# A norm's gain and bias loaded in turned form, and a pinned product moved ahead of `pv`

## The chip, the core and the metric

The kernel runs on one core of a Trainium2 chip. The metric is the device time of one execution in microseconds. The profile names the engines PE (TensorE, the matrix products), DVE (VectorE), ACT (ScalarE), POOL (GpSimd) and SP (SyncE, which issues most of the DMAs).

## The reference, cut to what matters

One encoder layer in float32: a state-space mixer and a gated MLP mixer over chunks of 128 positions, merged by gates; then cross-attention to a memory; then a SwiGLU feed-forward. The sequence has 512 rows of 1024 channels. The change touches the gated mixer's layer norm and the start of the feed-forward:

```python
def sgu_branch(zu, zv, ln_g, ln_b, w_s, bias):
    zu = jax.nn.gelu(zu)
    zv = layer_norm(jax.nn.gelu(zv), ln_g, ln_b)
    zv = zv.reshape(bsz, seq // CHUNK, CHUNK, SGU_HEADS, SGU_HEAD_DIM)
    sv = jnp.einsum('hts,bnshd->bnthd', w_s, zv) + bias.T[None, None, :, :, None]
    return zu * sv.reshape(bsz, seq, SGU_WIDTH)

def swiglu(hn, w_gate, w_up, w_down):
    return (jax.nn.silu(hn @ w_gate) * (hn @ w_up)) @ w_down
```

The mixing is linear, so the kernel applies the norm's gain `g` and bias `b` after it: `sv` is `g` times the mixed, normalised rows plus `mix`, and `mix` is `b` times the row totals of `w_s` plus `bias`. `g` and `b` have 1024 values each, 8 heads of 128 channels.

## The kernel before

**Products.** Each float32 weight is split in a high part `whi` (ScalarE, L85) and a low part `wlo` (DVE, L86), and each product is made of three: high-high, high-low, low-high (`mm3`, L376). Weights come in 512 KB blocks in a fixed list, `plan`; a block's load is issued three blocks ahead of its use (on SP's queue), and its split two blocks ahead. Tiles in PSUM are `pf` (products by features), `pt` (by tokens) and, in the feed-forward, `px`, `pv`, `pq`: the 256-column parts of products that are computed with seven instead of eight half-size products (`product`, L1252, 24 instructions each).

**Order.** Each engine runs its instructions in the order in which they stand in its own queue. That order is made when the kernel is built, by a scheduler that follows a modelled timeline; `in_order` pins an instruction to its place among the others so pinned, and `later(n, f)` writes a piece of code n ticks of product work further on. The order may therefore change far from an edit.

**The state-space side.** From 60 to 134 us, between the large products of `w_in`, each of eight groups goes the same way (`s5_inputs`, L948): DVE makes an operand in `wsx` (L983 twice, L987), PE turns it in two pieces `pw` (L961), ScalarE copies them to `wt`, PE multiplies them in one piece `pz` (L968; the trace shows each of the eight products as two matmuls), and ScalarE (L973) and DVE (L974) copy its two halves to `zh`. `pw`, `pz` and other small pieces share the PSUM pool `aux`, which has three banks (L81): a piece can begin when the piece three before it has been read. Then follows a scan on DVE (L992).

**Mixing.** The row totals of `w_s` (L1186) go through DRAM and come back as a broadcast to all partitions, `rsb`, which lies in the tile `squares` (L1190). `g` and `b` are loaded as 16 rows `gbr`, turned by PE (`pgb`) and copied to `gbc`, 128 partitions by 16. Eight DVE instructions (L1176) then make `mix` from `rsb`, `gbc` and the loaded bias; `psv` and `sv` (L1211) use it.

**Start of the feed-forward.** `gate_part` multiplies the rest of `w_gate` with the halves T0 and T1 of the tokens; `unit_start` and `unit_second` make `px` and `pv` of the first unit. `idle_product` (L1265) is one matmul whose result nobody reads, pinned behind `pv`.

Of the kernel before, what the change touches and what calls it, by code (L numbers as in the profile page):

```python
# [9 lines left out]
F32 = mybir.dt.float32  # L10
# [7 lines left out]
P = 128  # L18
# [11 lines left out]
H = 8  # L30
# [22 lines left out]
def hybrid_layer_kernel(  # L53
# [8 lines left out]
    nc = tc.nc  # L62
    x, mem, out = x[0], mem[0], out[0]
# [7 lines left out]
    np_ = ctx.enter_context(tc.tile_pool(name="norm", bufs=2))  # L71
# [5 lines left out]
    def bank(name):  # L77
        return pm.tile([P, 512], F32, tag="mm", name=name)

    def aux(name, shape=(P, 512)):  # L80
        return pa.tile(list(shape), F32, tag="aux", name=name)  # L81
# [12 lines left out]
    in_order = tc.keep_in_program_order  # L94
# [256 lines left out]
    def next_w(*key):  # L351
        i = used_w[0]
        used_w[0] += 1
        assert len(plan[i][0]) == len(key) and plan[i][0][1:] == key[1:] and plan[i][0][0] is key[0]
        for j in range(i, min(i + FAR + 1, len(plan))):
            begin(j, i)
            if j - 1 >= len(tiles) and j - 1 <= i + SPLITS:
                split_w(j - 1)
        for j in range(len(tiles), min(i + SPLITS + 1, len(plan))):
            split_w(j)  # L360
        tile_, tiles[i] = tiles[i], None
        return tile_
# [45 lines left out]
    def feat_block(ps, x, act, nk, kpt, tsl, fresh=True):  # L408

        kb, hi, lo = x  # L410
        for j in range(2):
            cs = slice(j * P, (j + 1) * P)
            for k in range(kpt):
                kk = kb + k
                mm3(ps[j][:, tsl], (hi[:, k, cs], lo[:, k, cs]), (act[0][:, kk, tsl], act[1][:, kk, tsl]),
                    kk == 0 and fresh, kk == nk - 1, not fresh)
# [45 lines left out]
    def later(n, fn):  # L462

        side["later"].append((side["now"] + n, fn))
# [7 lines left out]
    def tick(us=5.2):  # L472

        side["now"] += us / 5.2
        run_due()
        side["credit"] = min(side["credit"] + us * side["rate"], us)
        while side["credit"] > 0.0 and side["gen"] is not None:
            try:
                used = next(side["gen"])
            except StopIteration:  # L480
                side["gen"] = None
                return
            if used is None:
                side["credit"] = 0.0
                return
            side["credit"] -= used
# [8 lines left out]
    ident = cp.tile([P, P], F32, name="ident")  # L495
# [67 lines left out]
    def slot(tag, shape, dt, name, place=NEAR):  # L563
        n = math.prod(shape[1:])
        t = sp.tile([P, KD * T + ROOM[tag]], dt, tag=tag, name=name)[:, place[tag]:place[tag] + n]
        return t.rearrange("p (a b c) -> p a b c", a=shape[1], b=shape[2]) if len(shape) == 4 else (
            t.rearrange("p (a b) -> p a b", a=shape[1]))

    def token_slot(name, place=NEAR):
        return tuple(slot(tag, (P, KD, T), F32R, name, place) for tag in "BC")  # L570
# [584 lines left out]
        nc.scalar.activation(z, z, AF.Identity, bias=nm, scale=r)  # L1155

    nc.sync.dma_start(wsr, sgu_w[0].rearrange("h t s -> t h s"))
    gbr = np_.tile([2 * H, P], F32, tag="gain", name="gbr", bufs=2)
    nc.sync.dma_start(gbr[0:H, :], sgu_ln_g[0].rearrange("(h d) -> h d", d=P))
    nc.sync.dma_start(gbr[H:2 * H, :], sgu_ln_b[0].rearrange("(h d) -> h d", d=P))  # L1160
    mix = np_.tile([P, H, P], F32, tag="gain", name="mix", bufs=2)
    nc.sync.dma_start(mix, sgu_bias[0].rearrange("h t -> (h t)").partition_broadcast(P))

    def mixing_setup():
        for q in range(2):
            ps = aux("pws", (P, 4, P))
            for j in range(4):
                nc.tensor.transpose(ps[:, j, :], wsr[:, 4 * q + j, :], ident)
            nc.scalar.copy(wst[:, 4 * q:4 * q + 4, :], ps)
        ps = aux("pgb", (P, 2 * H))  # L1170
        nc.tensor.transpose(ps, gbr, ident[:2 * H, :2 * H])
        gbc = np_.tile([P, 2 * H], F32, tag="gbc", name="gbc", bufs=1)
        nc.vector.tensor_copy(gbc, ps)

        for h_ in range(H):
            nc.vector.scalar_tensor_tensor(mix[:, h_, :], rsb[:, :, h_], gbc[:, H + h_:H + h_ + 1], mix[:, h_, :],  # L1176
                                           ALU.mult, ALU.add)
        return gbc

    rsd = dp.tile([P, H], F32, name="rsd")  # L1180
    rsb = squares[:, 3, :].rearrange("p (t h) -> p t h", h=H)
# [14 lines left out]
        nc.scalar.activation(z, ps, AF.Sigmoid)  # L1196
        gads.append(nc.sync.dma_start(gad[m - OFF_GA // P], z))

    gbcs = []
    later(2.5, row_totals)  # L1200
    later(4, spread_totals)
    later(6, lambda: gbcs.append(mixing_setup()))
    for i in range(NT):
        later(1 + i, lambda i=i: layer_norm(i))
    for c0 in range(OFF_GA, OFF_GB, 256):
        feat(w_in, c0, xn, KD, ga_evac)


    gbc = gbcs[0]
    sv = slot("A", (P, H, T), F32, "sv")  # L1210
    for h in range(H):  # L1211
        ps = bank("psv")
# [12 lines left out]
    K0, K1, T0, T1 = slice(0, 4), slice(4, 8), slice(0, 256), slice(256, 512)  # L1225
# [26 lines left out]
    def product(ps, u, q, start, ops):  # L1252

        hi, lo = next_w(u[0], u[1], q)
        for j in range(2):
            cs = slice(j * P, (j + 1) * P)
            for k in range(4):
                a = (hi[:, k, cs], lo[:, k, cs])
                b = (ops[q][0][:, k, :], ops[q][1][:, k, :])
                for i, (x, y) in enumerate(((0, 0), (0, 1), (1, 0))):  # L1260
                    nc.tensor.matmul(ps[:, j, :], a[x], b[y], start=start and j == k == i == 0,  # L1261
                                     stop=k == 3 and i == 2, skip_group_check=True)
        tick(2.7)

    def idle_product(x, y):  # L1265

        in_order(nc.tensor.matmul(aux("idle"), x[:, 0, 0:P], y[:, 4, :], start=True, stop=True))

    def unit_bank(name):
        return bank(name).rearrange("p (j t) -> p j t", j=2)  # L1270
# [149 lines left out]
    h = slot("A", (P, NT, D), F32, "h")  # L1420
# [201 lines left out]
    fn_hi, fn_lo = token_slot("fn", AWAY)  # L1622
# [3 lines left out]
    ps = {t: bank(f"pt{t}") for t in range(NT)}  # L1626
# [45 lines left out]
    held, ps = [], {}  # L1672
# [70 lines left out]
    ops = {1: fn_q(K0, T0), 2: fn_q(K1, T0), 7: fn_q(K0, T1), 4: fn_q(K1, T1)}  # L1743

    def unit_start(u):
        x, v = unit_bank("px"), unit_bank("pv")
        product(x, u, 1, True, ops)
        nc.scalar.copy(v, x)
        return x, v

    def put(u, f, ts, src):
        dst = acts(u[1] // 512, f)[:, :, ts]
        if u[0] is w_gate:
            nc.scalar.activation(dst, src, AF.Silu)
        else:
            nc.vector.tensor_tensor(dst, dst, src, ALU.mult)

    def unit_second(u, v):
        product(v, u, 2, False, ops)
        put(u, 0, T0, v)  # L1760
# [3 lines left out]
    ps = [bank("pf0"), bank("pf1")]  # L1764
    ws = []

    def gate_part(i, ts):
        if ts is T0:
            ws.append((4 * i,) + next_w(w_gate, 4 * i, 4, FS, 256))
        feat_block(ps, ws[i], fn, KD, 4, ts, ts is T0)  # L1770
        tick(2.7)

    gate_part(0, T0)
    begun = unit_start(UNITS[0])
    gate_part(1, T0)
    unit_second(UNITS[0], begun[1])
    idle_product(ops[1][0], fn_hi)
    for i in range(2):
        gate_part(i, T1)
    for j in range(2):  # L1780
# [51 lines left out]
    for i, u in enumerate(UNITS):  # L1832
        final = i == len(UNITS) - 1
        x, v = begun
# [196 lines left out]
```

## Time and profile before

| what | value |
|---|---|
| median of three runs | 861.35 us (860.9 to 861.78) |
| the profiled execution | 861.22 us |
| its span, first to last instruction | 859.4 us |
| mean granted TensorE clock | 0.999 |
| busy: PE, DVE, ACT, POOL | 852.4, 663.6, 465.6, 86.1 us |
| DMA, mean over the span | 199 GB/s |

Busy time says how much of the span an engine worked; only an engine that others wait for sets the time. A row of a timeline has the start in us, the duration, engine, line, operation, output and inputs, and how many; in brackets stands how long the engine was idle before it and what ended that. A row of the list of DMAs has the count, the size of one and the median time from issue to landing.

### The profile page before, as it was taken

To read this page: it belongs to the slowest core of one execution; us is meant where nothing else is said; L and a number is where in the kernel's file an instruction comes from. 1 tells how busy PE (TensorE), PEld (TensorE's weight loads), DVE (VectorE), ACT (ScalarE), POOL (GpSimd) and SP (SyncE) were. 2 spreads that over 40 slices of the span, in tenths; PEclk is the share of its full clock that TensorE was granted. 3 is DMA by queue.
4 is the path that set the end of the run, shared out by engine and by line. 5 is a ranking of instruction groups with operands and counts; after the bars stand their busy time and mean duration, and the time that the engine had idled before them with its cause. 6 is when DMAs were issued, how large, how long until landed. Compare 5 with 4: busy or idle time off the path is not lost.

```text
span 859.4 us, 14731 instructions
## 1 busy us (share of the span) xinstructions
PE 852.4 (99%) x5760; PEld 764.2 (89%) x5760; DVE 663.6 (77%) x1078; ACT 465.6 (54%) x698; POOL 86.1 (10%) x119
## 2 busy tenths in 40 slices
PE   9999999999999999999999999999999999999997
PEld 6888888888889988899899888999999999988886
DVE  7898898899646867678758656867877768899876
ACT  6834953244455534457557444645545554655674
POOL 0002102211021111010010001010211111000000
PEclk9999999999999999999999999999999999999999
DMA  9879566888575798635696455567999898366664
GB/s 268 221 246 248 138 177 158 230 207 201 140 220 166 260 313 262 210 110 196 215 275 162 137 153 142 147 167 186 212 237 235 213 228 218 99 188 211 193 189 162
DMA packets 116200, 170.61 MB, mean 199 GB/s; under 512 B 9489, under 2 KB 80801, under 8 KB 116002
## 3 DMA queue, kind: packets, MB, share of 16 engines
q1 hardware_dynamic: 95778, 140.51, 50.1%
q0 software_dynamic: 20064, 28.55, 20.6%
q8 instruction: 45, 0.74, 0.3%
q10 hardware_dynamic: 288, 0.61, 0.2%
q14 instruction: 25, 0.20, 0.1%
HBM read 160.75 MB, written 48.73 MB: 244 GB/s over the span
## 4 chain that ended last, share of the span: by engine, by line
PE 98%; ACT 1%; DMA 1%; DVE 0%; SPq 0%; issue 0%
PE pf L379 27%; PE pt L379 17%; PE px L1261 13%; PE pq L1261 6%; PE dx L379 5%; PE dq L379 5%; PE pv L1261 3%; PE bx L1261 3%; PE qx L1261 3%; PE dv L379 2%; PE pz L968 2%; PE qv L1261 1%; PE po L379 1%; PE psc L379 1%; PE py L1025 1%; PE qq L1261 1%
## 5 line engine op out<-in xcount | busy, mean ns | idle before, releaser
L85 ACT CAST whi<-wraw 128x1024 fp32r<-128x1024 f32 x141 | 145.3, 1031 | 161.9 <-PE pf L379 61.1
L86 DVE TENSOR_TENSOR wlo<-wraw,whi 128x1024 fp32r<-128x1024 f32 x141 | 168.2, 1195 | 54.7 <-ACT whi L85 53.8
L379 PE MATMUL pf<-xn,whi 128*128 128x512 f32 x448 | 139.4, 392 | 0.0
L379 PEld LDWEIGHTS pf<-xn,whi 128*128 128x128 f32 x448 | 83.4, 188 | 16.8 <-issue 0.2
L379 PE MATMUL pf<-xn,wlo 128*128 128x512 f32 x224 | 87.7, 392 | 0.0
L1261 PE MATMUL px<-fn,whi 128*128 128x256 f32 x480 | 83.5, 277 | 0.0
L1261 PEld LDWEIGHTS px<-fn,whi 128*128 128x128 f32 x480 | 72.5, 188 | 0.2
L86 DVE TENSOR_TENSOR wlo<-b,whi 128x1024 fp32r<-128x1024 f32 x40 | 48.9, 1222 | 26.0 <-ACT whi L85 26.0
L85 ACT CAST whi<-b 128x1024 fp32r<-128x1024 f32 x40 | 42.2, 1054 | 47.9 <-PE px L1261 27.7
L1261 PE MATMUL px<-fn,wlo 128*128 128x256 f32 x240 | 66.4, 277 | 0.0
L1261 PE MATMUL pq<-s,whi 128*128 128x256 f32 x320 | 55.0, 276 | 0.0
L86 DVE TENSOR_TENSOR wlo<-t,whi 128x1024 fp32r<-128x1024 f32 x30 | 36.7, 1224 | 19.5 <-ACT whi L85 19.5
L85 ACT CAST whi<-t 128x1024 fp32r<-128x1024 f32 x30 | 31.6, 1054 | 36.2 <-PE pv L1261 13.3
L379 PEld LDWEIGHTS pf<-xn,wlo 128*128 128x128 f32 x224 | 42.0, 188 | 9.0 <-issue 0.2
L1261 PEld LDWEIGHTS pq<-s,whi 128*128 128x128 f32 x320 | 48.2, 188 | 0.0
L1261 PEld LDWEIGHTS px<-fn,wlo 128*128 128x128 f32 x240 | 45.1, 188 | 0.0
L1261 PE MATMUL pq<-s,wlo 128*128 128x256 f32 x160 | 44.2, 276 | 0.0
L379 PE MATMUL pt<-whi,xn 128*128 128x512 f32 x128 | 43.4, 404 | 0.0
L379 PE MATMUL dx<-whi,s 128*128 128x512 f32 x132 | 41.4, 390 | 0.0
L379 PE MATMUL dq<-whi,s 128*128 128x512 f32 x122 | 38.0, 389 | 0.0
L294 POOL DMA_DIRECT2D dsum<-in_w_down_dram x12 | 13.3, 1105 | 171.4 <-DMA dsum<-in_w_down_dram 166.5
L1261 PEld LDWEIGHTS pq<-s,wlo 128*128 128x128 f32 x160 | 30.1, 188 | 0.0
(456 smaller groups left out, 2221.7 us busy)
## 6 DMA issues: line engine op xcount, KB each, us to landing
wraw<-in_w_in_dram SPq DMA_DIRECT2D x34, 512.0 KB, 5.3
dsum<-in_w_down_dram SPq DMA_DIRECT2D x20, 512.0 KB, 5.8
wraw<-dsum SPq DMA_DIRECT2D x20, 512.0 KB, 3.7
b<-in_w_gate_dram SPq DMA_DIRECT2D x15, 512.0 KB, 5.1
b<-in_w_up_dram SPq DMA_DIRECT2D x15, 512.0 KB, 4.6
wraw<-in_w_down_dram SPq DMA_DIRECT2D x15, 512.0 KB, 4.4
dsum<-in_w_down_dram POOLq DMA_DIRECT2D x10, 512.0 KB, 7.8
dsum<-dsum POOLq DMA_DIRECT2D x10, 512.0 KB, 8.2
```

Of the source, the lines that this page charges most:

```text
L85: hi = nc.scalar.copy(dst_hi, src)
L86: lo = nc.vector.tensor_tensor(dst_lo, src, dst_hi.bitcast(F32), ALU.subtract)
L294: plan[j + step][1].append((0, lambda d=dst, x=more: nc.gpsimd.dma_start(d, x, accum_op=ALU.add)))
L379: m = nc.tensor.matmul(ps, a[x], b[y], start=start and i == 0, stop=stop and i == 2, skip_group_check=free)
L968: nc.tensor.matmul(ps[:, g, :], wt[:, g, :], u[:, o * GO + g, :], start=True, stop=True)
L1025: in_order(nc.tensor.matmul(ps[64 * j:64 * j + 64, :, :, h, :].rearrange("p q d c -> p d q c"), a, b, start=k == ks[0], stop=k == ks[2], t ...
L1261: nc.tensor.matmul(ps[:, j, :], a[x], b[y], start=start and j == k == i == 0, stop=k == 3 and i == 2, skip_group_check=True)
```

## The change

`g` and `b` are loaded directly in the form of `gbc`, 128 partitions by 8 values of 4 bytes each, by two DMAs; the 16-row tile `gbr`, its transpose on PE and the copy on DVE are gone. In the feed-forward, `idle_product` stands ahead of `unit_second`, that is ahead of `pv`; its moving operand was one slice of 512 tokens, and is now two slices of 256 tokens of T0.

```diff
-    gbr = np_.tile([2 * H, P], F32, tag="gain", name="gbr", bufs=2)
-    nc.sync.dma_start(gbr[0:H, :], sgu_ln_g[0].rearrange("(h d) -> h d", d=P))
-    nc.sync.dma_start(gbr[H:2 * H, :], sgu_ln_b[0].rearrange("(h d) -> h d", d=P))
+    gbc = np_.tile([P, 2 * H], F32, tag="gbc", name="gbc", bufs=1)
+    nc.sync.dma_start(gbc[:, 0:H], sgu_ln_g[0].rearrange("(h d) -> d h", d=P))
+    nc.sync.dma_start(gbc[:, H:2 * H], sgu_ln_b[0].rearrange("(h d) -> d h", d=P))
...
-        ps = aux("pgb", (P, 2 * H))
-        nc.tensor.transpose(ps, gbr, ident[:2 * H, :2 * H])
-        gbc = np_.tile([P, 2 * H], F32, tag="gbc", name="gbc", bufs=1)
-        nc.vector.tensor_copy(gbc, ps)
...
-        return gbc
...
-    later(6, lambda: gbcs.append(mixing_setup()))
+    later(6, mixing_setup)
...
-        in_order(nc.tensor.matmul(aux("idle"), x[:, 0, 0:P], y[:, 4, :], start=True, stop=True))
+        in_order(nc.tensor.matmul(aux("idle", (P, 2, 256)), x[:, 0, 0:P], y, start=True, stop=True))
...
     begun = unit_start(UNITS[0])
     gate_part(1, T0)
+    idle_product(ops[1][0], fn_hi[:, 4:6, T0])
     unit_second(UNITS[0], begun[1])
-    idle_product(ops[1][0], fn_hi)
```

The first place is DVE's queue at the seventh of the eight state-space groups. The names in brackets are the semaphores that an instruction waits for (DMAHW: a DMA). Before:

```order
L1154 TENSOR_TENSOR nm<-nm,r 128x1 [waits Pool_49]
L86 TENSOR_TENSOR wlo<-wraw,whi 128x1024 [waits DMAHW2_49,PE_49,Activation_49]
L983 TENSOR_TENSOR wsx<-bbr,pw_441 128x1024 [waits PE_49]
L974 COPY zh<-pz 64x8x64 [waits Activation_49]
L987 TENSOR_TENSOR wsx<-wsx,etmp_1172 128x1024 [waits DVE_49]
L983 TENSOR_TENSOR etmp_1176<-bbi,pw_441 128x1024 [waits DVE_49]
```

And now:

```order
L1154 TENSOR_TENSOR nm<-nm,r 128x1 [waits Pool_49]
L86 TENSOR_TENSOR wlo<-wraw,whi 128x1024 [waits DMAHW2_49,PE_49,Activation_49]
L1172 SCALAR_TENSOR_TENSOR mix<-squares,gbc,mix 128x128 [waits DMAHW6_49]
L1172 SCALAR_TENSOR_TENSOR mix<-squares,gbc,mix 128x128 x7
L983 TENSOR_TENSOR wsx<-bbr,pw_441 128x1024 [waits PE_49]
L974 COPY zh<-pz 64x8x64 [waits Activation_49]
L987 TENSOR_TENSOR wsx<-wsx,etmp_1172 128x1024 [waits DVE_49]
L983 TENSOR_TENSOR etmp_1176<-bbi,pw_441 128x1024 [waits DVE_49]
```

The eight sums stood behind the start of the scan, some forty rows further on; they now stand in the middle of this group, and the first waits for a DMA.

The second place is PE's queue at the same groups: the turns `pw`, the products `pz` and the large products `pf` around them. Before:

```order
L961 MATMUL pw<-ident,wsx 128x128 [waits Activation_49]
L961 MATMUL pw<-ident,wsx 128x128 x3
L968 MATMUL pz<-u,wt 128x64 [waits DVE_49]
L968 MATMUL pz<-u,wt 128x64 x7
L379 MATMUL pf_1184<-xn,whi 128x512 x2
L379 MATMUL pf_1184<-xn,wlo 128x512
```

And now:

```order
L961 MATMUL pw<-ident,wsx 128x128 [waits Activation_49]
L961 MATMUL pw<-ident,wsx 128x128 x3
L379 MATMUL pf_1184<-xn,whi 128x512 x2
L379 MATMUL pf_1184<-xn,wlo 128x512
L968 MATMUL pz<-u,wt 128x64 [waits DVE_49]
L968 MATMUL pz<-u,wt 128x64 x7
```

Three products of `pf` have moved ahead of this `pz`. Further on the new order places three more behind the next `pz` pieces, and has `pw` and `pz` there in fours with three `pf` between.

The third place is PE's queue at the start of the feed-forward. Before:

```order
L1261 MATMUL pv<-fn,whi 128x256 x2
L1261 MATMUL pv<-fn,wlo 128x256
L1267 MATMUL idle<-fn 128x512 [waits PE_49,Activation_49]
L379 MATMUL pf_5648<-fn,s_5464 128x256
L379 MATMUL pf_5648<-fn,s_5464 128x256 [waits DVE_49]
```

And now:

```order
L379 MATMUL pf_5645<-fn,s_5646 128x256 x12
L1260 MATMUL idle<-fn 128x512 [waits Activation_49]
L1254 MATMUL pv<-fn,whi 128x256 [waits Activation_49]
L1254 MATMUL pv<-fn,whi 128x256
L1254 MATMUL pv<-fn,wlo 128x256
```

The pinned product stands ahead of the 24 `pv` products now, with nothing else moved there. On SP's queue the two loads keep their place, behind that of `w_s` (L1157) and ahead of that of `mix` (L1162).

More of the change, by code (lines that the diff above doesn't have):

```diff
@@ L1197, in ga_evac @@
         gads.append(nc.sync.dma_start(gad[m - OFF_GA // P], z))
-    gbcs = []
     later(2.5, row_totals)
     later(4, spread_totals)
-    later(6, lambda: gbcs.append(mixing_setup()))
+    later(6, mixing_setup)
     for i in range(NT):
@@ L1206, in hybrid_layer_kernel @@
         feat(w_in, c0, xn, KD, ga_evac)
-    gbc = gbcs[0]
     sv = slot("A", (P, H, T), F32, "sv")
```

## The prediction

> **What bounds the kernel now.** I read the page first: its busy times and the chain that ended last.
>
> ```profile
> span 859.4 us, 14731 instructions
> PE 852.4 (99%) x5760; PEld 764.2 (89%) x5760; DVE 663.6 (77%) x1078; ACT 465.6 (54%) x698; POOL 86.1 (10%) x119
> PE 98%; ACT 1%; DMA 1%; DVE 0%; SPq 0%; issue 0%
> ```
>
> TensorE is busy for 852.4 of 859.4 us, and 98% of the chain is its own. Second, the waits of PE, which are all that it has:
>
> ```profile
> PE pt L582 <- DVE ones L498: 1.1, 1, 1.1
> PE pt L379 <- DVE wlo L660: 0.3, 1, 0.3
> ```
>
> Both lie at the start. So the time is the sum of PE's products. An edit gains only what it takes off PE, and costs whatever makes PE wait where it never waited. Third, therefore, the timelines of PE and DVE around each place that the order of instructions shows as changed.
>
> **The pinned product.** It is one 512-column product before and after; only its place moves, ahead of the 24 products `pv`. PE's timeline there, with start and duration:
>
> ```profile
> 544.01 0.40 PE L1261 MATMUL pv<-fn,whi 128*128 128x256 f32 x2
> ...
> 546.84 0.39 PE L1267 MATMUL idle<-fn 128*128 128x512 f32 x1
> 547.07 5.61 PE L379 MATMUL pf<-fn,s 128*128 128x256 f32 x48
> 552.51 0.39 PE L379 MATMUL pf<-fn,whi 128*128 128x256 f32 x2
> ```
>
> The 24 `pv` take 546.84 - 544.01 = 2.83 us, 118 ns each; the 48 products behind the pinned one take 552.51 - 547.07 = 5.44 us, 113 ns each. The pinned product changes PE's pace by 4%. If it does the same from its new place, `pv` gains 24 x 4.6 ns = 0.11 us, and the products behind `pv` stay at 113. If the two-part operand doesn't restore the pace, the gain is nothing and the 48 products lose 48 x 4.6 = 0.22. I take -0.11: it has the same 512 columns. Its new wait costs nothing, because the `pv` behind it waits for ScalarE in any case.
>
> **The turn that goes.** PE's timeline at the removed transpose:
>
> ```profile
> 138.95 0.23 PE L1171 MATMUL pgb<-ident,gbr 16*128 16x16 f32 x1
> 139.11 0.73 PE L379 MATMUL pf<-xn,whi 128*128 128x512 f32 x2
> ```
>
> PE's step there is 139.11 - 138.95 = 0.16 us: -0.16. The DVE copy of 0.18 us goes too, off the path.
>
> **The sums that move.** The eight `mix` sums no longer need PE's transpose, so the order puts them far ahead on DVE, right behind a `wlo` and ahead of `wsx` (L983). They read `rsb`, the broadcast of the row totals (L1190), and wait for its DMA. Did it land by then? Rows of DVE, of SP's queue and of tile `squares`:
>
> ```profile
> 105.98 1.22 DVE L86 TENSOR_TENSOR wlo<-wraw,whi 128x1024 fp32r<-128x1024 f32 x1
> 107.13 1.22 DVE L983 TENSOR_TENSOR wsx<-bbr,pw 128x1024 f32<-128x1024 f32 x1
> 108.38 1.08 DVE L974 COPY zh<-pz 64x512 f32<-64x512 f32 x1
> 109.50 1.23 DVE L987 TENSOR_TENSOR wsx<-wsx,etmp 128x1024 f32<-128x1024 f32 x1
> ...
> 112.94 1.23 DVE L983 TENSOR_TENSOR wsx<-bbr,pw 128x1024 f32<-128x1024 f32 x1 [0.96 <-PE pw L961]
> ...
> 120.07 1.07 DVE L974 COPY zh<-pz 64x512 f32<-64x512 f32 x1
> ...
> 140.68 3.02 DVE L1176 SCALAR_TENSOR_TENSOR mix<-squares,gbc,mix 128x128 f32<-128x128 f32 x8
> 143.60 0.23 DVE L999 TENSOR_TENSOR zh<-sa,sb 128x64 f32<-128x64 f32 x1
> ```
>
> ```profile
> 104.83 0.38 SPq L1190 DMA_DIRECT2D squares<-rsd  x1
> ```
>
> ```profile
> DMA to landing us min/median/max: 5.2/5.2/5.2
> ```
>
> The broadcast is issued at 104.83 and lands 5.2 us later, at 110.03. DVE reaches the new place of the sums at 107.13 and would stand there for 2.9 us. The sums take 143.60 - 140.68 = 2.92 us, from about 110.1 to 113.05. So the `wsx` of 107.13 starts at 113.05, and everything queued behind it on DVE is 5.9 us late. Nothing ahead of this place changes on DVE, SP, ScalarE or PE but the two small loads at 25 us, so I take these times over.
>
> Who waits for DVE? Rows of PE:
>
> ```profile
> 111.87 1.03 PE L961 MATMUL pw<-ident,wsx 128*128 128x128 f32 x8
> 112.74 1.90 PE L968 MATMUL pz<-u,wt 128*128 128x64 f32 x16
> 114.44 0.71 PE L379 MATMUL pf<-xn,whi 128*128 128x512 f32 x2
> 114.99 0.40 PE L379 MATMUL pf<-xn,wlo 128*128 128x512 f32 x1
> 115.22 0.62 PE L379 MATMUL pf<-xn,whi 128*128 128x512 f32 x2
> ...
> 116.61 1.89 PE L968 MATMUL pz<-u,wt 128*128 128x64 f32 x16
> 118.34 0.61 PE L961 MATMUL pw<-ident,wsx 128*128 128x128 f32 x4
> ...
> 123.37 1.00 PE L968 MATMUL pz<-u,wt 128*128 128x64 f32 x8
> 124.20 0.28 PE L961 MATMUL pw<-ident,wsx 128*128 128x128 f32 x1
> ```
>
> The `pz` of 112.74 takes the PSUM bank of the `pz` three pieces before it (the pool has three), and waits until DVE's copy `zh` (L974) has read that one. The copy ends at 108.38 + 1.08 = 109.46 now, 3.3 us before it is needed; 5.9 later is 115.36. In the new order three `pf` products of 0.23 us stand ahead of this `pz`, so PE is there at 112.74 + 0.68 = 113.42. Wait: 115.4 - 113.4 = **1.97 us**. The `pw` of 118.34 is safe: its operand (L987) ends at 110.73 now and at 116.6 then, and PE is later than that by its own wait.
>
> A second wait follows. From 113.05 on DVE has no idle time (the 0.96 us ahead of 112.94 is eaten up), and the copy of 120.07, which ends at 121.14, comes 121.14 - 107.13 - 0.96 = 13.05 us of work behind 113.05: at 126.1. The `pw` of 124.20 needs the bank that it frees. PE's work between the two waits was 124.20 - 112.74 = 11.46 us; six `pf` products have left it (three now stand before, three behind), 1.36 us, so PE is there at 115.4 + 10.1 = 125.5 and waits **0.6 us**.
>
> Then the debt is repaid: at 140.68 DVE no longer has 2.92 us of sums to do, so it is 5.9 - 0.96 - 2.92 = 2.0 us late there, and PE as late as it. I expect no further wait. The new order also cuts `pf` into two more runs between `pw` and `pz`; the first pair of a run takes 0.71 instead of 0.62, so with its slow start some 0.1 each, **+0.2 us**.
>
> **The loads.** Two 4 KB loads of 8 rows of 512 B become 2 x 1024 pieces of 4 B. The nearest rows are SP's and the DMA list's: `dcol` is also loaded in pieces of 4 B, 128 at a time, and `crow` in 512 pieces of 256 B.
>
> ```profile
> 23.09 1.45 SPq L844 DMA_DIRECT2D dcol<-in_s_d_dram  x3
> 24.59 0.43 SPq L1157 DMA_DIRECT2D wsx<-in_sgu_w_dram  x1
> ...
> 27.25 3.36 SPq L145 DMA_DIRECT2D wraw<-in_w_in_dram  x2
> ```
>
> ```profile
> wraw<-in_w_in_dram SPq DMA_DIRECT2D x34, 512.0 KB, 5.3
> ...
> crow<-in_s_c_re_dram SPq DMA_DIRECT2D x2, 128.0 KB, 6.5
> ...
> dcol<-in_s_d_dram SPq DMA_DIRECT2D x4, 0.5 KB, 3.6
> ```
>
> ```profile
> 38.15 1.04 ACT L85 CAST whi<-wraw 128x1024 fp32r<-128x1024 f32 x1
> ```
>
> SP spends 0.48 us to issue a `dcol` piece and 0.43 to issue `wsx` in its 1024 pieces, so the issue costs what it did. Landing: 3.6 us at the least; at the most, taking `crow`'s 6.5 us twice for twice the pieces, 13 us each, 26 if the two follow each other. `gbc` is first read at 110 us. Queued behind are `mix` and then the weights of 27.25, which land at 32.6 and are cast at 38.15: 5.5 us to spare. I take nothing, from `dcol`, which is the only one with pieces of 4 B; the upper end, 26 - 5.5 = 20 us less what PE still has in hand, is for a rival. [...]
>
> **Sum**, against the profiled execution (span 859.4, 861.22 with what lies around it; the median of the three runs is 861.35, so 0.13 above it): -0.11 - 0.16 + 1.97 + 0.6 + 0.2 = +2.5. **863.7 us.** A measurement of this kernel can tell about 0.2% (1.7 us) from no change.
>
> **The rivals.**
>
> 1. *The sums find their broadcast landed* (not slower). If it lands by 107.2, DVE is only 2.92 us late, the copy ends at 112.4, before PE's 113.4, and the 0.96 us in hand covers most of the rest. Then the time is 861.22 - 0.11 - 0.16 + 0.2 = 861.2. Each us by which the landing moves, moves the end by a us, and below 107.2 it decides nothing more. Against it: 5.2 us to landing must become 2.4. The DMA list's other 512 KB broadcasts:
>
> ```profile
> g_x<-in_xattn_norm_g_dram SPq DMA_DIRECT2D x1, 512.0 KB, 9.1
> g_o<-in_final_norm_g_dram SPq DMA_DIRECT2D x1, 512.0 KB, 4.6
> ```
>
> None lands so soon; 4.6 would give 863.1. 0.15.
>
> 2. *The broadcast lands later*, as `g_x` did: 3.9 us more, up to 867.6. The issue at 104.83 waits for nothing that changes, and its neighbours in the queue are the same, so 0.1. [...]
>
> 3. *The small pieces hold SP's queue* beyond the 5.5 us in hand; PE then waits for `whi` between 40 and 60 us, and the time is 863.7 plus up to 20 us. `dcol` speaks against it. 0.05.
>
> **How the numbers follow.** The forecast has 0.7, with the landing at 4.6 to 6 us: 863.1 to 864.6. Adding rival 1 down to 861.2 and the nearer part of rival 2, the range is 861.2 to 866.0, and leaves out the far parts of rivals 2 and 3 and a little of rival 1: under 0.15. Slower by over 0.2% (over 863.1): nearly all of the forecast and rivals 2 and 3, less some for landings at the lower end, 0.77. Within 0.2%: most of rival 1 and that lower end, 0.19. Faster: PE's products offer less than 0.3 us, 0.04.
>
> **What would show it.** In the trace after: ahead of `mix` (L1172) DVE idle for about 2.9 us on a DMA, near 107 to 110; among PE's waits two new ones on DVE's `zh`, about 2.0 us at `pz` (L968) and 0.6 at `pw` (L961); no `pgb`; `pv` at 113 ns a product; `gbc` issued in under 1 us each. I am wrong if PE's waits are as short as before, if `whi` or `wlo` make PE wait in the first 60 us, or if PE waits elsewhere, which the order then didn't tell.

## The result, and the profile after

| | median | lowest to highest | executions |
|---|---|---|---|
| before | 861.46 us | 860.71 to 863.03 | 17 |
| after | 863.16 us | 862.77 to 869.69 | 17 |

The changed kernel is slower: its median is 1.70 us higher (0.20%), and the ratio, in which the long executions count, is 1.0036 (95% interval 1.0024 to 1.0048), which is some 3 us. Its 17 executions fall into two groups: 12 lie between 862.77 and 864.2 us at a granted TensorE clock of 0.998 to 1.0, and 5 between 866.66 and 869.69 us at 0.992 to 0.994. The profiled execution, 869.38 us, is one of the long ones. A second series of the same kernel, first among the experiments, gave a profile of the short group, 862.93 us; both are read here, and sizes are compared with the forecast in the short one.

The page of after: the span, and the granted clock in 40 slices.

```profile
span 867.6 us, 14722 instructions
PEclk9999979999999999999999999999999999999999
```

In before it stands at nine tenths or more in every slice:

```profile
PEclk9999999999999999999999999999999999999999
```

In after the clock dips in the sixth slice, 108 to 130 us: the place of the moved sums. DVE and PE there:

```profile
106.84 1.23 DVE L86 TENSOR_TENSOR wlo<-wraw,whi 128x1024 fp32r<-128x1024 f32 x1
111.42 3.02 DVE L1172 SCALAR_TENSOR_TENSOR mix<-squares,gbc,mix 128x128 f32<-128x128 f32 x8 [3.36 <-DMA squares<-rsd]
114.35 1.23 DVE L983 TENSOR_TENSOR wsx<-bbr,pw 128x1024 f32<-128x1024 f32 x1
115.61 1.02 DVE L974 COPY zh<-pz 64x512 f32<-64x512 f32 x1
```

```profile
112.44 1.03 PE L961 MATMUL pw<-ident,wsx 128*128 128x128 f32 x8
...
113.78 0.40 PE L379 MATMUL pf<-xn,wlo 128*128 128x512 f32 x1
116.68 3.56 PE L968 MATMUL pz<-u,wt 128*128 128x64 f32 x16 [2.51 <-DVE zh L974]
120.00 1.20 PE L379 MATMUL pf<-xn,whi 128*128 128x512 f32 x2
```

This is the forecast chain, link by link: DVE stands 3.36 us in front of the sums until the broadcast lands, does 3 us of sums, and only then reaches the `zh` copy for which PE's `pz` waits, 2.51 us. But the work behind the wait is slow as well. The 16 `pz` matmuls take 3.56 us where before they took 1.90, and two `pf` products 1.20 instead of 0.71. Why, the windows of 2 us show (the length, the busy time of PE, of PE's weight loads (PEld), of DVE, ACT and POOL, each with its count, then the granted clock, the DMA share and GB/s):

```profile
114.00:116.00 2.00, 0.17 (x1) 0.00 (x0) 1.97 (x4) 0.42 (x1) 1.03 (x1) 1.00 0.32 14
116.00:118.00 2.00, 1.32 (x7) 1.32 (x7) 1.94 (x3) 0.00 (x0) 0.00 (x0) 0.71 0.92 124
118.00:120.00 2.00, 2.00 (x11) 2.00 (x11) 2.00 (x2) 0.00 (x0) 0.00 (x0) 0.50 0.81 128
...
126.00:128.00 2.00, 2.00 (x8) 1.62 (x7) 1.94 (x3) 0.60 (x3) 0.00 (x0) 0.73 0.00 0
128.00:130.00 2.00, 2.00 (x13) 1.65 (x12) 1.93 (x3) 1.01 (x2) 0.00 (x0) 1.00 0.33 126
```

If the clock is either full or half, as in the windows at 1.00 and 0.50, 0.71 over 2 us is 1.16 us at a half, so the half clock begins at 116.84; 0.73 is 1.08 us, so it ends at 127.08. PE is busy all through them, so these 10.24 us at half speed cost about 5.1 us, an estimate. With the wait of 2.51 they make 7.6 of the 8.16 us by which this execution is longer than the profiled one of before. About as much as the rest was there ahead of this place: PE reaches this `pw` at 112.44 here and at 111.87 in before.

The same place in the short execution (second series), DVE and PE:

```profile
109.30 3.02 DVE L1172 SCALAR_TENSOR_TENSOR mix<-squares,gbc,mix 128x128 f32<-128x128 f32 x8 [2.78 <-DMA squares<-rsd]
```

```profile
111.84 1.03 PE L961 MATMUL pw<-ident,wsx 128*128 128x128 f32 x8
...
114.56 2.00 PE L968 MATMUL pz<-u,wt 128*128 128x64 f32 x16 [0.99 <-DVE zh L974]
...
125.20 0.66 PE L961 MATMUL pw<-ident,wsx 128*128 128x128 f32 x4 [0.27 <-DVE zh L974]
```

Here both forecast waits are seen, 0.99 and 0.27 us, and the clock stays full.

The loads in after, on SP's queue, and the time from issue to landing of `gbc`:

```profile
25.63 0.70 SPq L1159 DMA_DIRECT2D gbc<-in_sgu_ln_g_dram  x1
26.37 1.23 SPq L1160 DMA_DIRECT2D gbc<-in_sgu_ln_b_dram  x1
27.65 1.80 SPq L1162 DMA_DIRECT2D mix<-in_sgu_bias_dram  x1
29.55 1.68 SPq L145 DMA_DIRECT2D wraw<-in_w_in_dram  x2
```

```profile
DMA to landing us min/median/max: 4.7/4.9/5.1
```

A load of 1024 pieces of 4 bytes takes 0.70 and 1.23 us to issue and lands 5 us later, 80 us before anyone reads it. In before the two loads took 0.63 and 0.28 us, and `mix` behind them 0.36 instead of 1.80. The weights behind these are issued at 29.55 instead of 27.25, 2.3 us later, but PE doesn't wait for them: its waits in after are those of before and the one at `pz`.

### The profile page after: what moved, and what is told of

Its sections match the earlier page's. It is cut to its first block, busy times and chain, and to the rows that moved or that the text cites. A ratio compares the mean times of both kernels' runs of the same rounds, so it can differ in the third digit from the quotient of the medians.

```text
span 867.6 us, 14722 instructions
## 1 busy us (share of the span) xinstructions
PE 858.0 (99%) x5759; PEld 769.2 (89%) x5759; DVE 663.9 (77%) x1077; ACT 465.4 (54%) x698; POOL 86.4 (10%) x119
## 4 chain that ended last, share of the span: by engine, by line
PE 92%; DVE 3%; ACT 2%; DMA 2%; issue 1%; SPq 0%; DVEq 0%
PE pf L379 25%; PE pt L379 15%; PE px L1254 13%; PE pq L1254 6%; PE dx L379 5%; PE dq L379 5%; PE pv L1254 3%; PE bx L1254 3%; PE qx L1254 3%; PE dv L379 2%; PE qv L1254 1%; PE po L379 1%; PE py L1025 1%; PE psc L379 1%; PE qq L1254 1%; PE bq L1254 1%
## 5 line engine op out<-in xcount | busy, mean ns | idle before, releaser
L379 PE MATMUL pf<-xn,whi 128*128 128x512 f32 x448 | 141.2, 396 | 0.0
```

Source lines behind the costliest of these rows:

```text
L379: m = nc.tensor.matmul(ps, a[x], b[y], start=start and i == 0, stop=stop and i == 2, skip_group_check=free)
```

## The experiments

The theory: the eight sums, at their new place, make DVE wait for the broadcast, and PE for DVE; all else in the change, but for the runs of `pf` that are cut, is worth about -0.3 us. The rivals: the four-byte loads cost the time; the pinned product does; 2.9 us of DVE work at this place are enough without any wait. Each series has its own runs of before on the same chip.

### The changed kernel again (after_again)

> The changed kernel, unchanged, for a second profiled execution and more times. Theory (the eight early sums make VectorE wait for the broadcast, and TensorE for VectorE): about +1.6 us against before in executions at full clock, with a TensorE wait of 2 to 2.5 us at the pz products near 114 us; in roughly 3 of 10 executions that gap also sets the granted clock to a half for about 10 us, and the time is 5 to 6 us longer still. If this profile is at full clock, it shows whether the second wait that was forecast (0.6 us at the pw transposes) is there. Rival (the half clock belongs to the chip and not to this kernel): before, run beside it, shows the same long executions as often.

Measured: 863.54 us median (862.71 to 869.39, 12 executions), before 861.76 (860.97 to 862.53, 29); ratio 1.0038 (1.0022 to 1.0054). Four of the 12 are long, 867.56 to 869.39, at a clock of 0.992 to 0.994; none of the 29 of before has a clock below 0.998. The half clock comes with this kernel and not with the chip. The wait at `pz` in the profile at full clock is 0.99 us, and not the 2 to 2.5 that I had expected; the second wait, 0.27, is there. Over both series 20 executions at full clock have a median of 863.15, 9 at the lower clock 868.38.

### The loads alone, and the pinned product alone (gb_only, idle_only)

```diff
 # gb_only: the hunks on gbr, pgb and gbc, without those on idle_product
 # idle_only: these alone
-        in_order(nc.tensor.matmul(aux("idle"), x[:, 0, 0:P], y[:, 4, :], start=True, stop=True))
+        in_order(nc.tensor.matmul(aux("idle", (P, 2, 256)), x[:, 0, 0:P], y, start=True, stop=True))
...
+    idle_product(ops[1][0], fn_hi[:, 4:6, T0])
     unit_second(UNITS[0], begun[1])
-    idle_product(ops[1][0], fn_hi)
```

> Before with the four-byte loads of g and b alone; the idle product is as before. The sums move ahead on VectorE as in the changed kernel. Theory: the same wait at pz and the same time as the changed kernel, 862.8 to 863.6 at full clock, and executions with the clock at a half among them; pv at 118 ns. Rival (the idle product costs the time): as before, 861.4.

> Before with the idle product alone changed (two rows of 256 columns, ahead of pv); g and b are loaded and turned as before. Theory: the 24 pv products take 113 ns in place of 118, 0.11 us, and nothing else moves: 861.2 to 861.5, within what can be told from before. Rival (the idle product costs the time): 862.5 or more.

Measured: gb_only 865.23 us (862.9 to 868.58, 6 executions), ratio 1.0043 (1.0026 to 1.006), two executions with a clock of 0.993 and 0.994; idle_only 861.61 (860.98 to 862.52, 11), ratio 0.9999 (0.9991 to 1.0008). The loss comes with `g` and `b`. Of the four executions of gb_only at full clock only 862.9 is in the range that I gave, 862.8 to 863.6; 863.98, 865.04 and 865.42 are longer, at a clock of 0.998 to 0.999. They have no profile, so it isn't shown whether they had a longer wait at `pz` or something else. The profiled execution, 867.07 us: DVE, PE and the windows.

```profile
110.63 3.02 DVE L1172 SCALAR_TENSOR_TENSOR mix<-squares,gbc,mix 128x128 f32<-128x128 f32 x8 [3.13 <-DMA squares<-rsd]
```

```profile
112.14 1.03 PE L961 MATMUL pw<-ident,wsx 128*128 128x128 f32 x8
...
115.89 2.02 PE L968 MATMUL pz<-u,wt 128*128 128x64 f32 x16 [2.02 <-DVE zh L974]
```

```profile
116.00:118.00 2.00, 2.00 (x17) 2.00 (x18) 1.97 (x2) 0.06 (x1) 0.00 (x0) 0.93 1.17 180
118.00:120.00 2.00, 2.00 (x8) 1.71 (x8) 2.00 (x3) 0.99 (x1) 0.00 (x0) 0.50 0.37 58
...
124.00:126.00 2.00, 2.00 (x9) 1.54 (x9) 1.94 (x3) 0.67 (x2) 0.00 (x0) 0.86 0.01 2
```

By the same arithmetic the half clock lasts from 117.72 to 124.56 here, 6.84 us. The pinned product, in idle_only and in gb_only:

```profile
545.03 0.39 PE L1261 MATMUL pv<-fn,whi 128*128 128x256 f32 x2
...
547.76 5.49 PE L379 MATMUL pf<-fn,s 128*128 128x256 f32 x47
```

```profile
549.83 0.40 PE L1254 MATMUL pv<-fn,whi 128*128 128x256 f32 x2
...
552.66 0.39 PE L1260 MATMUL idle<-fn 128*128 128x512 f32 x1
```

With the product moved ahead, the 24 `pv` take 547.76 - 545.03 = 2.73 us, 114 ns each; where it stays behind, 2.83, 118 each. The gain of 0.1 us is in the trace and far below what the times can tell.

### The sums held back (sums_held)

`behind(a, b)` tells the scheduler to place instruction `a` behind instruction `b`.

```diff
             st["kept"] = V.tensor_copy(zv[hi_], ps[hi_, :, ::-1])
+            st["last_kept"] = st["kept"]
...
+    def mixing_sums():
         for h_ in range(H):
-            nc.vector.scalar_tensor_tensor(mix[:, h_, :], rsb[:, :, h_], gbc[:, H + h_:H + h_ + 1], mix[:, h_, :],
+            m = nc.vector.scalar_tensor_tensor(mix[:, h_, :], rsb[:, :, h_], gbc[:, H + h_:H + h_ + 1], mix[:, h_, :],
...
+            behind(m, st["last_kept"])
...
+    later(7.5, mixing_sums)
```

> The changed kernel with one thing undone: the eight mix sums are held behind the last zh copy, which puts them near 135 us, past the zh copies that TensorE waits for; the four-byte loads and the idle product ahead of pv stay. Theory (the place of the sums is the whole loss): no wait for the broadcast, no new TensorE wait, no half clock in any execution, and 0.1 to 0.3 us less than before, 861.1 to 861.4. Rival (the four-byte loads cost the time, or the idle product does): still 1 us or more slower than before.

Measured: 861.08 us (860.78 to 862.15, 11 executions) beside 861.76 of before; ratio 0.9995 (0.9986 to 1.0003). DVE in its profile, and PE's waits, all of them:

```profile
106.82 1.23 DVE L984 TENSOR_TENSOR wsx<-bbr,pw 128x1024 f32<-128x1024 f32 x1
108.08 1.08 DVE L974 COPY zh<-pz 64x512 f32<-64x512 f32 x1
...
135.10 3.02 DVE L1174 SCALAR_TENSOR_TENSOR mix<-squares,gbc,mix 128x128 f32<-128x128 f32 x8
```

```profile
PE pt L582 <- DVE ones L498: 1.1, 1, 1.1
PE pt L379 <- DVE wlo L660: 0.3, 1, 0.3
```

The four-byte loads and the moved product are still in it, and the whole loss is gone: it was the place of the sums. The rival of the loads falls. PE's order at the groups is that of before again, so this run alone doesn't part the sums from the runs of `pf` that are cut; the next one does.

### The work without the wait, and a later wait (bcast_early, bcast_late)

```diff
 # bcast_early
-        behind(nc.sync.dma_start(rsb, rsd.rearrange("t h -> (t h)").partition_broadcast(P)), gads[0])
+        nc.sync.dma_start(rsb, rsd.rearrange("t h -> (t h)").partition_broadcast(P))
...
+            behind(m, scaled[-1])               # m: each sum; scaled: nm <- nm, r (L1154)
 # bcast_late
-        behind(nc.sync.dma_start(rsb, rsd.rearrange("t h -> (t h)").partition_broadcast(P)), gads[0])
+        behind(nc.sync.dma_start(rsb, rsd.rearrange("t h -> (t h)").partition_broadcast(P)), gads[1])
```

> The changed kernel with the broadcast of the row sums issued right behind their store, near 88 us in place of 104 to 106, so that it has landed long before the eight sums; the sums are held behind the last scaling of the layer norm and stay where the changed kernel has them on VectorE, ahead of the wsx product and the zh copy. This parts the wait for the broadcast from the 2.9 us of VectorE work. Theory (the wait is the cause, and the work alone is covered): VectorE goes without a wait, TensorE has none at pz above 0.3 us, the clock stays at full in every execution, 861.0 to 861.5. Rival (2.9 us of work ahead of the zh copy is enough by itself): a TensorE wait of 1 us or more at pz stays, 862 or more.

> The changed kernel with the broadcast held behind the second store of gas on SyncE's queue in place of the first: it is issued some 1.5 us later, and the order of VectorE changes with it, so that the eight sums stand behind the next zh copy, wsx sum and etmp product, about 4.7 us of work later. Theory (what counts is that the zh copy does not queue behind the wait): VectorE reaches the sums near 113 us, the broadcast lands near 111, no wait at pz, 861.0 to 861.6, although the broadcast comes later. Rival (the landing of the broadcast sets the time, wherever the sums stand): 1.5 us longer than the changed kernel, 864 or more.

Measured: bcast_early 861.54 us (860.93 to 862.92, 11 executions) beside 861.53, ratio 1.0 (0.9992 to 1.0009); bcast_late 861.06 (860.59 to 861.5, 11), ratio 0.9994 (0.9985 to 1.0003). DVE in bcast_early:

```profile
105.28 3.04 DVE L1172 SCALAR_TENSOR_TENSOR mix<-squares,gbc,mix 128x128 f32<-128x128 f32 x8
108.24 1.21 DVE L86 TENSOR_TENSOR wlo<-wraw,whi 128x1024 fp32r<-128x1024 f32 x1
...
110.62 1.08 DVE L974 COPY zh<-pz 64x512 f32<-64x512 f32 x1
```

```profile
113.31 1.89 PE L968 MATMUL pz<-u,wt 128*128 128x64 f32 x16
```

The 3 us of sums stand ahead of the `zh` copy as in after, one `wlo` earlier. The copy ends at 111.7, and PE's `pz` begins at 113.31 without a wait, although only one `pf` product stands ahead of it, where after has three. The loss needs the wait; the work alone is covered. And in bcast_late:

```profile
108.61 1.08 DVE L974 COPY zh<-pz 64x512 f32<-64x512 f32 x1
...
113.02 2.96 DVE L1172 SCALAR_TENSOR_TENSOR mix<-squares,gbc,mix 128x128 f32<-128x128 f32 x8 [0.81 <-DMA squares<-rsd]
```

The broadcast lands 1.6 us later than in the profile of after (the sums begin at 113.02 instead of 111.42), and the kernel is about 2 us faster: the order now has the sums behind the copy that PE needs, and their wait holds up nobody. I had expected the landing near 111 and no wait of DVE; PE has none at `pz`, as expected. A second series asked whether it beats before:

> The changed kernel with the broadcast held behind the second store of gas, a second time, on whatever chip comes: it was 0.5 us below before with an interval that just takes in no difference. Theory (the idle product ahead of pv and the missing transpose are worth 0.27 us together, and nothing is lost): 0.1 to 0.6 us below before. Rival (the first result was chance): as before or above it.

It gave 861.44 us (860.51 to 862.7, 11 executions) beside 861.45, ratio 0.9998 (0.9989 to 1.0007). So bcast_late and sums_held beat the changed kernel by 1.7 to 2.5 us, each beside its own runs of before; that they beat before isn't shown.

### Other lengths of the gap (sums_early_4, bcast_delayed)

```diff
 # sums_early_4: the code of sums_held, for the last four sums only
+    later(6, lambda: mixing_sums(range(4), False))
+    later(7.5, lambda: mixing_sums(range(4, H), True))
 # bcast_delayed: ahead of the broadcast in the changed kernel
+        for i in range(2):
+            spare = dp.tile([P, H], F32, name="spare%d" % i)
+            behind(nc.sync.dma_start(spare, rsd), gads[0])
```

> The changed kernel with four of the eight sums left where it puts them, behind the wait for the broadcast, and four held behind the last zh copy: VectorE is 1.5 us less late at the zh copy. Theory: TensorE waits at pz 0.8 us less than in the changed kernel (the order there also loses one run of pf ahead of pz), 0.2 to 1.7 us from execution to execution; about 862.2 and, if the clock falls only after a gap of about 2 us or more, no execution above 864. Rival (the clock falls after any such gap): executions of 866 and more about as often as in the changed kernel, 9 of 29 so far.

> The changed kernel with two small copies of the row sums (4 KB each, from one place in memory to another) issued on SyncE's queue right ahead of the broadcast, which delays it by two issues, 0.7 to 0.9 us. Six of the eight sums stand one wsx product later on VectorE, still ahead of the zh copy; TensorE has one run of pf products more ahead of its pz products, 0.7 us of cover. Theory (the gap on TensorE is what lets the clock fall, and its length varies from execution to execution): the gap at pz is about 0.2 us longer than in the changed kernel, 1.2 to 2.9 us, so executions at full clock near 863 to 864.5, and executions of 866 to 871 at least as often as in the changed kernel (9 of 29). Rival (the clock falls by chance, whatever the gap): the share of such executions is unchanged or lower, and they occur in before as well.

Measured: sums_early_4 861.79 us (861.35 to 866.59, 12 executions), ratio 1.0007 (0.9997 to 1.0017), with one execution of 866.59 at a clock of 0.995, where I had expected none. bcast_delayed 862.45 (861.6 to 866.75, 11), ratio 1.0018 (1.0005 to 1.0031), with two at 0.994 and 0.995, 866.25 and 866.75. PE in the two profiles, both at a granted clock of 1.0:

```profile
113.84 2.00 PE L968 MATMUL pz<-u,wt 128*128 128x64 f32 x16 [0.25 <-DVE zh L974]
```

```profile
115.00 2.00 PE L968 MATMUL pz<-u,wt 128*128 128x64 f32 x16 [0.64 <-DVE zh L974]
```

In bcast_delayed I forecast the gap too long, 1.2 to 2.9 us. Its DVE is where that of the short profile of after is: the `wlo` ahead of the sums starts at 105.30 and 105.29. The two copies do delay the issue of the broadcast, to 105.4 from 104.15, but it lands after 4.4 us and not 5.1, so the sums begin only 0.43 us later, at 109.73. PE comes to its `pw` 0.35 us later (112.19 against 111.84) and has two more `pf` products, of some 0.23 us each, ahead of `pz`: 0.8 us in all. The PE wait of 0.64 us is shorter than the three seen with the sums in the place where the change puts them. So it is a second, unintended, shorter gap and not the longer one that I wanted; the longer side wasn't tried. Its long executions are fewer than the changed kernel's (2 of 11, against 9 of 29), as are those of sums_early_4 (1 of 12), though on small counts. The five series without a gap (sums_held, idle_only, bcast_early and both of bcast_late) have 55 executions, and before 79 beside them: none has a clock under 0.998. The half clock comes with the gap; how long the gap was in each of the long executions isn't known, but for the two that have a profile.

## Why the prediction was right, and what it left out

- **The place of the sums, +1.97 us at `pz`: right in kind and in the middle of its spread.** DVE idle 2.9 us forecast, 2.78 to 3.36 seen; the sums 2.92 forecast, 2.9 seen. The size of PE's wait differs from profile to profile, 0.99, 2.02 and 2.51, and follows one rule: the sums begin 2.54, 1.51 and 1.02 us before PE's `pw` (111.84 - 109.30, 112.14 - 110.63, 112.44 - 111.42), and each time this lead and the wait add up to 3.53. So what I took from one profile as a number, the broadcast's landing against PE's progress, is a quantity that moves by 1.5 us between executions, and PE waits for each us of it, as rival 1 said. The broadcast was issued at 104.15, 105.12 and 105.69 in these three and landed after 5.1, 5.5 and 5.7 us; PE was later too, but by 0.6 us only. The forecast of 1.97 took both from one execution of before.
- **The second wait, +0.6 at `pw`:** 0.27 in the short profile, absent in the two long ones (after, gb_only), where PE itself was late by then.
- **The sum, in part by luck:** the short profile has waits of 1.26 us in place of the forecast 2.57, and the 12 short executions have a median of 863.02, 1.56 above before in place of 2.5; the long ones are 5.2 us and more above it. Ten of these 12 lie below 863.3; only 863.71 is at the forecast 863.7. The mechanism was right; that the median came within 0.54 us owes something to the long executions, which move it up, and to before, which measured 861.46 and not 861.22.
- **Two more runs of `pf`, +0.2:** PE's `psv` products began at 153.00 in before and at 154.39 in the short profile of after:

```profile
153.00 7.31 PE L1214 MATMUL psv<-wsx,zt 128*128 128x128 f32 x64
```

```profile
154.39 7.30 PE L1207 MATMUL psv<-wsx,zt 128*128 128x128 f32 x64
```

  These 1.39 us are the waits, 1.26, less the transpose, 0.16, and 0.29 for the rest, the runs of `pf` among it. Behind `psv` this execution loses another 0.3 us of the 1.71 by which it is longer than before's (862.93 against 861.22); no run says to what.
- **The pinned product, -0.11:** 2.73 us instead of 2.83 in the trace, for 24 `pv`. **The transpose, -0.16:** no `pgb` in the trace, and nothing shows that contradicts the term.
- **The loads at nothing:** right in the time, wrong in a step. Both bounds of the landing, 3.6 and 13 us, hold the 5 us that were seen. That the issue costs what it did is wrong: 0.70 and 1.23 us instead of 0.63 and 0.28, and `mix` behind them 1.80 instead of 0.36. The 5.5 us that the weights had to spare took it up. Why the issue is longer isn't shown; whatever is slow about these loads is hidden here, as sums_held shows (861.08 us with them, 861.76 for before beside it).
- **What the sum left out: the clock.** No term of the sum stands for it. In the two profiles it fell behind gaps of 2.02 and 2.51 us, and took some 3.4 and 5.1 us, an estimate (half of 6.84 and of 10.24); it fell in 9 of 29 executions of the changed kernel and in 2 of 6 of gb_only. The median didn't notice, because two thirds of the executions keep the full clock: 863.16 against 863.7. The range, up to 866.0, missed the long ones.

## To carry to other kernels

When an edit takes away an instruction's last local dependency, ask what it will wait for next and who queues behind it: here a copy that PE needed stood behind sums that nobody needed for 40 us. An order made from a modelled timeline put the sums where, in every profile, their DMA had not landed; three cures worked, an ordering edge, an earlier DMA and even a later one. And the wait on TensorE cost twice in the profile of after: its own length, 2.51 us, and some 5.1 us, an estimate, at the half clock behind it.

## What the runs showed of the hardware

- The half clock lasted 10.24 us once (after) and 6.84 us once (gb_only), by the windows above. PE took up work again at 116.68 and 115.89, and by the same windows the clock fell 0.16 and 1.83 us later, at 116.84 and 117.72, an estimate; PE was busy from there to the end of the half clock. What sets the moment and the length stays open.
- A gap of 0.99 us, 0.64 or 0.25 in a profile left the clock alone: 0.999, 1.0 and 1.0 in these executions. Whether there is a limit, and on what else it depends, stays open; the execution of gb_only at 865.42 us, 3.7 above before at a clock of 0.999, may have had a longer gap that left the clock alone.
- A pinned 512-column product goes with a quicker pace of the 256-column products behind it: `pv` takes 118 ns each in the two profiles where the product stands behind it (before, gb_only) and 113 to 114 in those of after, after_again and idle_only, where it stands ahead, with an operand in two pieces. Why, no run says.
